# Strassen feed-forward layer: a fourth second-level product in block 0, twelve weight sums moved into block 1, and x of block 2 fetched sooner

## Chip, cores, metric

One NeuronCore of a Trainium2 chip. The metric is the device time of one execution in microseconds (us), the median over several executions. The reported time is some 2 us more than the span of the profile, which ends with the last instruction.

## The reference

```python
batch, m, k, h, n = 16, 512, 768, 3072, 768      # x, w1, b1, w2: normal draws, float32
def reference(x, w1, b1, w2):
    y = np.matmul(x, w1) + b1
    y = 0.5 * y * (1.0 + erf(y / np.sqrt(2.0)))   # exact gelu
    return np.matmul(y, w2).astype(np.float32)
```

The 8192 rows of x are worked in eight blocks of 1024.

## The kernel before

Operands are float16, sums are kept in float32. Every product is done by Strassen's scheme: seven products of half-sized operands in place of eight, for additions that VectorE does beside TensorE. The second products (`gelu(...) @ w2`) of blocks 2 to 7 use two levels of it. Blocks 0 and 1 run while W2 is still being prepared and use one level, with exceptions:

- A **plain unit** (`Unit2`) makes 128 rows of each half of the block's outputs: up to seven products, each of 12 matmuls of 384 columns. A block has four such units.
- A **second-level unit** (`UnitH`) does one whole first-level product of a block by seven products of its own, each of 12 matmuls of 192 columns. It needs sums of the left operand ("level sums", 1536 elements to a partition) and sums of W2's quarters (1152 elements to a partition, 288 KB each).
- In block 1 the first-level products 1, 4 and 2 were second-level units, and its four plain units are **lean**: they do only products 3, 5, 6 and 7.

All of on-chip memory is one tile, `arena`, cut by hand into regions that are reused as soon as their data are dead. So the profile names nearly every on-chip operand "arena", and the scheduler makes an instruction wait whenever it writes a region that an earlier instruction or transfer still uses. Only matmul banks in PSUM have names of their own: bX, bY, bZ, bW.

The sums of W2's quarters for blocks 2 to 7 are stored to DRAM once, in the time of blocks 0 and 1. A sum is written to a staging buffer by VectorE and stored from there by the SP queue:

```python
def split_w2(p, t=None, q=None):          # before: t picked from five staging buffers in turn
    b11, b12, b21, b22 = quarters(p)
    def put(q, src):
        nc.sync.dma_start(out=w2s[p, q][:], in_=src)
    ...
    for n, a, b in ((7, b22, b12), (5, b12, b11), (6, b22, t[5]), (4, b21, t[6])):
        def f(n=n, a=a, b=b):
            tt(t[n], a, b, SUB)                    # VectorE
            puts.append(lambda: put(n, t[n]))      # store, issued at the next slot
        later(WB, f, slow if q is None else q)
```

A unit is a sequence of seven products; between them "slots" 1 to 6 issue other work. The parts that the change touches:

```python
class Unit2:
    def mm(self, p, dst, first, c0, c1):
        if self.lean and p in (1, 2, 4):
            return
        ...
HYBRID = (1, 4, 2)                                 # second-level products, all of block 1
def p7(u):
    u.mm(7, bY[u.g % 2], False, 0, u.C)
    add_c22(u)                                     # VectorE: out row sum, reads bank bY
def p4(u):
    ...
    u.mm(4, bY[u.g % 2], False, 0, u.C)            # goes on in bY: must wait for add_c22
def fill_mm2_one(sb, U, slot):                     # block 0
    ...
            for p in (5, 6, 7, 3):
                split_w2(p)
            hyb_w[1] = split_w2(1)
def fill_hyb(sb, m, slot):                         # second-level units
    ...
    if slot == 6:
        flush(queue)
        if m == 2:
            load_next_x(2, range(3))               # x of block 2, POOL queue, float32 to float16
def fill_lean(sb, k, slot):                        # lean units of block 1
    ...
    if k == 0 and slot == 6:
        for t in range(3):
            transpose_dma(2, t)                    # SP queue
        load_next_x(2, range(3, 6))
    if k == 1 and slot == 2:
        for n in range(2):
            load_wt(2 * NH + n)                    # w1 tiles of block 2, SP queue
    ...
    if k == 3 and slot == 4:
        x_sums(2, soon)
```

## Time and profile before

| | before |
|---|---|
| median time | 852.79 us (852.54 to 854.39, 6 runs) |
| span of the profiled run | 850.6 us |
| matmuls | 6432, TensorE busy 845.5 us |
| block 0's second product to block 2's first matmul | 120.01 to 224.67 us: 104.66 us |
| mean granted clock of TensorE | 1.00 |

The last but one row is the stretch to which the change belongs. It is read as the start of the first matmul of 384 columns of block 0 and the start of the first matmul of 512 columns of block 2.

(Timeline: start, length, engine, line, operation, operands, count, and in brackets the idle time before it and what ended it.)

### The profile page before, as it was taken

Reading aid. Unit: us, or ns where it says so; the run is one execution under the profiler, and the core shown is the slowest. Engines: PE = TensorE matmul, PEld = TensorE weight load, DVE = VectorE, ACT = ScalarE, POOL = GpSimd, SP = SyncE. Lnnn points to the kernel's source line nnn. Section 1 sums busy time; section 2 is a strip of 40 time slices with the busy share of each in tenths; the row PEclk is TensorE's granted clock in tenths of the full one; section 3 lists DMA queues with packets and bytes.
Section 4 is the critical chain, followed back from the end, with each engine's and each line's share of the span. In section 5 each row is a group of like instructions: output and inputs, shape, how many; then the busy total and the mean of one; then the engine's idle time right before and its main releaser. Section 6 shows DMA issues by size and latency. Waiting matters only on the chain.

```text
span 850.6 us, 16487 instructions
## 1 busy us (share of the span) xinstructions
PE 845.5 (99%) x6432; PEld 569.6 (67%) x6432; DVE 667.2 (78%) x1126; ACT 421.3 (50%) x686; POOL 84.1 (10%) x135
## 2 busy tenths in 40 slices
PE   9999999999999999999999999999999999999998
PEld 5444446687544897449964499645995469944798
DVE  5766678786657998679976799768996699956998
ACT  4777761122277513773148822487216771267611
POOL 5021100002100002000020000210002100010000
PEclk9999999999999999999999999999999999999999
DMA  9998777659999699987999689995999949984398
GB/s 229 199 284 170 165 160 277 234 195 218 234 331 207 194 332 372 296 177 236 332 381 266 155 291 335 361 293 111 315 351 344 283 111 328 356 311 172 101 310 283
DMA packets 143522, 219.05 MB, mean 258 GB/s; under 512 B 61756, under 2 KB 84724, under 8 KB 143444
## 3 DMA queue, kind: packets, MB, share of 16 engines
q1 hardware_dynamic: 117824, 179.74, 67.3%
q0 software_dynamic: 25440, 38.15, 20.6%
q8 instruction: 50, 0.82, 0.4%
q14 instruction: 28, 0.23, 0.1%
q10 hardware_dynamic: 180, 0.11, 0.0%
HBM read 180.30 MB, written 47.87 MB: 268 GB/s over the span
## 4 chain that ended last, share of the span: by engine, by line
PE 95%; DMA 4%; DVE 0%; ACT 0%; issue 0%; POOL 0%; DVEq 0%; ACTq 0%
PE bY L388 21%; PE bY L493 15%; PE bX L388 14%; PE bX L493 10%; PE bZ L388 7%; PE bW L388 7%; PE bZ L493 5%; PE bW L493 5%; PE bY L432 5%; DMA arena<-in_x_dram 2%; PE bZ L432 2%; PE bW L432 2%; PE bX L432 2%; DMA arena<-in_w_dram 1%; PE bY L580 1%; PE bX L580 1%
## 5 line engine op out<-in xcount | busy, mean ns | idle before, releaser
L191 DVE TENSOR_TENSOR arena<-arena 128x768 f16<-128x768 f16 (+4 forms) x630 | 403.4, 671 | 7.5 <-PE bW L432 1.1
L388 PEld LDWEIGHTS <-arena 128*128 128x128 f16 x1974 | 192.6, 98 | 224.0 <-issue 0.4
L493 PEld LDWEIGHTS <-arena 128*128 128x128 f16 x3528 | 292.1, 98 | 8.4 <-issue 0.4
L388 PE MATMUL bY<-arena 128*128 128x512 f16 x846 | 214.4, 379 | 0.1
L613 DVE TENSOR_TENSOR arena<-bY,arena 128x512 f32<-128x512 f32 (+1 forms) x102 | 69.4, 681 | 127.0 <-PE bY L388 90.3
L493 PE MATMUL bY<-arena 128*128 128x192 f16 x1500 | 138.3, 246 | 0.0
L388 PE MATMUL bX<-arena 128*128 128x512 f16 x564 | 138.2, 379 | 0.0
L606 ACT COPY bY<-bX 128x512 f32<-128x512 f32 (+1 forms) x143 | 78.6, 550 | 119.4 <-DVE arena L542 82.0
L404 ACT ACTIVATE arena<-arena,b1t 128x1024 f16<-128x1024 f32 x94 | 108.0, 1149 | 54.0 <-DVE arena L641 54.0
L626 ACT COPY arena<-bW 128x512 f32<-128x512 f32 (+1 forms) x147 | 81.1, 552 | 90.7 <-PE bW L493 43.9
L493 PE MATMUL bX<-arena 128*128 128x192 f16 x1020 | 93.1, 246 | 0.1
L641 DVE TENSOR_TENSOR arena<-bZ,arena 128x512 f32<-128x512 f32 (+1 forms) x102 | 69.3, 679 | 22.2 <-PE bZ L388 18.2
L388 PE MATMUL bW<-arena 128*128 128x512 f16 x282 | 76.2, 379 | 0.0
L388 PE MATMUL bZ<-arena 128*128 128x512 f16 x282 | 76.2, 379 | 0.0
L432 PEld LDWEIGHTS <-arena 128*128 128x128 f16 x528 | 51.6, 98 | 34.1 <-issue 0.2
L525 POOL DMA_DIRECT2D out_dram<-arena x42 | 30.6, 729 | 406.4 <-DVE arena L637 370.2
L409 ACT ACTIVATE arena<-bX,b1t 128x512 f16<-128x512 f32 x94 | 64.0, 681 | 10.0 <-PE bX L388 10.0
L409 ACT ACTIVATE arena<-bY,b1t 128x512 f16<-128x512 f32 x94 | 63.4, 674 | 0.0
L657 ACT COPY bZ<-bY 128x512 f32<-128x512 f32 (+1 forms) x54 | 29.0, 537 | 65.7 <-DVE arena L641 31.4
L299 POOL DMA_DIRECT2D arena<-in_x_dram x60 | 32.7, 550 | 248.2 <-DMA arena<-arena 137.9
L493 PE MATMUL bW<-arena 128*128 128x192 f16 x504 | 48.4, 246 | 0.0
L493 PE MATMUL bZ<-arena 128*128 128x192 f16 x504 | 48.4, 246 | 0.0
(60 smaller groups left out, 401.8 us busy)
## 6 DMA issues: line engine op xcount, KB each, us to landing
arena<-w2s SPq DMA_DIRECT2D x294, 288.0 KB, 4.7
arena<-w1s SPq DMA_DIRECT2D x72, 672.0 KB, 7.0
out_dram<-arena POOLq DMA_DIRECT2D x42, 384.0 KB, 7.2
w2s<-arena SPq DMA_DIRECT2D x49, 288.0 KB, 3.8
arena<-in_x_dram POOLq DMA_DIRECT2D x60, 192.0 KB, 7.1
w1s<-arena SPq DMA_DIRECT2D x12, 672.0 KB, 6.1
arena<-in_w_dram POOLq DMA_DIRECT2D x17, 384.0 KB, 7.6
out_dram<-arena SPq DMA_DIRECT2D x17, 384.0 KB, 3.4
```

The lines of the kernel that those rows point to most:

```text
L191: nc.vector.tensor_tensor(out=o, in0=a, in1=b, op=op)
L299: nc.gpsimd.dma_start(out=xhs[t], in_=xr[:, sb * 8 + t, :])
L388: nc.tensor.matmul(out=dst[:, 0:RH], lhsT=w1_op(self.wt, slot)[:, c, :], rhs=a[:, c, :], start=first and c == 0, stop=c == self.C - 1, ski ...
L404: nc.scalar.activation(out=self.G[1][:, hi, :, :], in_=self.tmp, func=GELU, bias=b1t[:, 2 * hi + 1:2 * hi + 2])
L409: nc.scalar.activation(out=self.G[0][:, hi, row, :], in_=bank[:, 0:RH], func=GELU, bias=b1t[:, 2 * hi:2 * hi + 1])
L432: nc.tensor.matmul(out=dst[:, 0:N2], lhsT=a, rhs=w[:, :, c, :], start=first and c == 0, stop=c == self.C - 1, skip_group_check=True)
L493: nc.tensor.matmul(out=dst[:, t * N4:(t + 1) * N4], lhsT=a, rhs=w[:, c, :], start=first and c == 0 and t == ts[0], stop=c == NQ - 1, skip_ ...
L525: eng.dma_start(out=orr[:, s0:s0 + 2, right * N2:(right + 1) * N2], in_=self.dst[:, r].rearrange("p t h n -> p t (h n)"))
L606: nc.scalar.copy(out=bY[u.g % 2][:, 0:u.F], in_=bX[u.g % 2][:, 0:u.F])
L613: nc.vector.tensor_tensor(out=u.c22(), in0=bY[u.g % 2][:, 0:u.F], in1=w[:, 0:u.F], op=ADD)
L626: nc.scalar.copy(out=w[:, 0:u.F], in_=bW[:, 0:u.F])
L641: nc.vector.tensor_tensor(out=u.c12(), in0=bZ[:, 0:u.F], in1=w[:, 0:u.F], op=ADD)
```

## The change

The intent is fewer matmul columns: product 2 of block 0 becomes a second-level unit as well. To make room on VectorE in block 0, twelve of W2's 28 sums move into block 1's units. That costs staging memory: two of the sums' sets share two buffers, and six sums that the second-level units need are stored to DRAM and read back. x of block 2 comes sooner: in the program its first three loads stand two units sooner, its later loads and its transposes about one. Core of the diff:

```diff
-        HYBRID = (1, 4, 2)
+        HYBRID = ((0, 2), (1, 1), (1, 4), (1, 2))          # (block, product)
 # Unit2.mm
-                if self.lean and p in (1, 2, 4):
+                if p == 2 or self.lean and p in (1, 4):
 # p6: copy of a bank in block 0's units goes from VectorE to ScalarE
-            on_act = ... or (isinstance(u, Unit2) and u.lean) or ...
+            on_act = ... or isinstance(u, Unit2) or ...
 # fill_mm2_one (block 0)
-                    for p in (5, 6, 7, 3):
-                        split_w2(p)
-                    hyb_w[1] = split_w2(1)
+                    for p, t in ((6, (0, 1, 2, 3)), (1, (4, 5, 0, 1)), (4, (2, 3, 4, 5)), (2, (0, 1, 2, 5))):
+                        split_w2(p, t)
 # fill_hyb (second-level units)
+            if m == 0 and slot == 1:
+                load_w2s(1, (7, 4))                        # read back
+            if m == 1 and slot == 6:
+                split_w2(7, (6, 7, 6, 7))                  # buffers 6 and 7 for both sets
+                split_w2(5, (6, 7, 6, 7))
+            if (m, slot) in ((1, 6), (2, 1), (2, 3), (2, 5), (3, 1), (3, 4)):
+                slow.pop(0)[1]()                           # one sum of W2 each
+            if m == 2 and slot == 1:
+                load_w2s(4, (7, 4))
             if slot == 6:
                 flush(queue)
-                if m == 2:
+                if m == 1:
                     load_next_x(2, range(3))
+                if m == 3:
+                    for t in range(3):
+                        transpose_dma(2, t)
+                    load_next_x(2, range(3, 6))
 # fill_lean
+            if k == 0 and slot == 4:
+                LAG[0] = 3                                 # stores from here on: three slots after the sum
+                split_w2(3, (1, 2, 3, 4))
-            if k == 1 and slot == 4:
+            if k == 0 and slot == 6:
                 for t in range(3, 6):
                     transpose_dma(2, t)
                 load_next_x(2, range(6, 8))
-            if k == 2 and slot == 4:
+            if k == 1 and slot == 6:
                 for t in range(6, 8):
                     transpose_dma(2, t)
-            if k == 3 and slot == 4:
+            if k == 3 and slot == 3:
                 x_sums(2, soon)
 ...   # buffers' places, output rows split in two, hyb_lev (places of level sums)
```

## The prediction

> **What bounds the kernel now.** I read the page's first part, then the chain that ended last, then the busy time by stage around the second products of blocks 0 and 1 (120 to 225 us, where all of the change lies), then the pieces of the chain and VectorE's timeline there.
>
> ```profile
> PE 845.5 (99%) x6432; PEld 569.6 (67%) x6432; DVE 667.2 (78%) x1126; ACT 421.3 (50%) x686; POOL 84.1 (10%) x135
> ...
> PE 95%; DMA 4%; DVE 0%; ACT 0%; issue 0%; POOL 0%; DVEq 0%; ACTq 0%
> ```
> ```profile
> core 0: us, PE busy (x) PEld busy (x) DVE busy (x) ACT busy (x) POOL busy (x), PEclk, DMA share, GB/s
> 120.00:170.70 50.70, 50.70 (x311) 30.23 (x309) 39.51 (x57) 9.66 (x19) 0.00 (x0) 1.00 0.68 240
> 170.70:194.40 23.70, 23.70 (x253) 21.36 (x252) 20.09 (x28) 6.94 (x15) 1.61 (x3) 1.00 0.56 190
> 194.40:224.70 30.30, 30.30 (x207) 19.43 (x205) 19.18 (x27) 4.92 (x11) 6.71 (x12) 1.00 0.99 207
> ```
>
> TensorE carries 95% of the chain, and in all three stages (block 0's plain units, the three second-level units, the lean units of block 1) its busy time equals the stage. "Busy" overlaps and could hide gaps, so the chain, whose pieces follow each other, is the better proof:
>
> ```profile
> 170.86 0.99 PE bX L580 x12
> 171.85 1.95 PE bY L432 x12
> ...
> 193.54 0.99 PE bX L580 x12
> 194.53 1.02 PE bY L580 x12
> ...
> 224.84 0.65 PE bX L388 x3
> 225.48 2.01 PE bY L432 x12
> ```
>
> Twelve matmuls of 384 columns take 1.95 us (162.5 ns each), twelve of 192 take 0.99 us (82.5 ns). Every piece I compared has that length except two: the product before 195.56 is 0.03 long, the one at 225.48 is 0.06 long. So the region that the change touches holds about 0.1 us of stall. It is pure matmul streaming: time goes down only by the matmuls' columns, and up only by new waits.
>
> **What the Trainium skill says.** "TensorE: Matmul & The Clock Gate", section "Back-to-back issue gap", gives N/2.4 + 2.5 ns at full clock: 162.5 ns for 384 and 82.5 for 192, which is what this trace shows, at a granted clock of 1.00. Its other sentence there, that a stream of weight loads and matmuls of 512 columns sustains some 131 ns each, does not hold here: three of them take 0.65 us, 216 ns each. The same page's "Architectural detail" says VectorE and ScalarE are strict FIFO; so a VectorE sum that has to wait for a buffer holds up the PSUM additions behind it, which matters below. "DMA: Bandwidth & Descriptors", section "Anatomy of one DMA", gives a fixed part of about 2 us per transfer (measured on the GpSimd path); here a 288 KB store of a W2 sum from the SP queue takes 2.1 us at least and 3.7 at the median from 117 to 240 us.
>
> **The change, part by part.**
>
> (a) TensorE. Four plain units lose product 2: 4 x 12 matmuls of 384 columns = 48 x 162.5 = 7.80 us. The new second-level unit has 7 products of 6 x 2 matmuls of 192 columns = 84 x 82.5 = 6.93 us. Net -0.87 us, with 36 more matmuls (6432 to 6468). This is on the path and sure. Per matmul column the second level saves an eighth, but 84 fixed parts of 2.5 ns instead of 48 take back 0.09.
>
> (b) VectorE, rates from its timeline: a 1536-element f16 sum occupies it for 0.88 us (0.95 long, overlapping the next), a 1152-element sum 0.74, a 384-column PSUM addition 0.47. Added: four level sums of the left operand (3.5 us) and some eight small PSUM operations of the new unit; gone: four copies of a bank, which move to ScalarE (4 x 0.47 us; it is 19% busy there). The number of W2 sums is the same, 28 of 0.74 us, but twelve of them (products 7, 5, 3) now run in the units of block 1, five of these between 179 and 193 us. For a plain unit of now 6 x 1.95 = 11.7 us I count 4 operand sums, 6 W2 sums and 2 additions: 3.5 + 4.4 + 0.9 = 8.9 us, in the third unit 10.7 with two level sums. So block 0 has room.
>
> (c) DMA. Six pieces of W2 sums of 288 KB (four of product 1, two of product 4) are stored and read back for the second-level units: 1.7 MB more, in a stage with DMA share 0.56. Lateness counts only at first use. The tightest: product 1's piece 5 can be loaded only when the last plain unit has used its operand (product 3 ends at about 168.8 us), and is wanted 5.9 us later (0.99 + 1.95 + 3 x 0.99). Ahead of it on the queue are one addition (0.6), an output store and its own issue (0.35 each), then 3 to 4 to landing: 4.3 to 5.3 us, so it should just be hidden.
>
> (d) x of block 2 is loaded and transposed sooner, and x's sums go to slot 3 of the last lean unit. That can remove at most the 0.06 at 225.48.
>
> **Where a new wait could appear.** VectorE before, at the end of the second-level units:
>
> ```profile
> 192.46 0.55 DVE L637 TENSOR_TENSOR arena<-bZ,arena 128x384 f32<-128x384 f32 x1
> 192.93 0.95 DVE L191 TENSOR_TENSOR arena<-arena 128x1536 f16<-128x1536 f16 x1
> 193.79 0.56 DVE L654 TENSOR_TENSOR bZ<-bY,arena 128x384 f32<-128x384 f32 x1
> 194.57 0.56 DVE L542 TENSOR_TENSOR arena<-bX,arena 128x384 f32<-128x384 f32 x1 [0.22 <-PE bX L580]
> ```
>
> The addition at 193.79 has to end before TensorE writes bank bY again at 194.4: it is just late, the one 0.03 us stall. Afterwards the same point is at 193.5 us (0.87 sooner). Laying the new order out with the rates of (b): the chain of additions tied to matmuls releases VectorE at 188.75 us (the addition after the second product of the last unit but one); from there to the end of the critical addition stand three PSUM additions (the first at 188.75), one W2 sum, two operand sums and the critical addition itself: 4 x 0.47 + 0.74 + 2 x 0.88 + 0.1 = 4.5, ending at 193.2. Slack 0.3 us if no W2 sum waits for its staging buffer. But the sums of products 7 and 5 share two buffers, and each waits for the store of the last but one: a sum done at 183.05 is stored by 186.2 to 187.3, the next sum in that buffer can start then, and with the level sum behind it VectorE is free at 187.9 to 188.9 instead of 186.8. That just touches 188.75. So I expect a stall of 0 to 0.5 us there, 0.2 in the middle.
>
> **Rivals.**
>
> (1) The stores hold VectorE, and through it TensorE, at several points: 1 to 2 us of stall, which eats the gain: 852.5 to 853.5. For it: VectorE ran without a break from 185 to 190 us before, the stores wait in order on one SP queue behind output stores and read-backs, and two buffers replace five. Against: each sum has a slot of 2 to 3 products before the next use, and DMA is idle half of that stage.
>
> (2) A read-back is late: TensorE waits at the second unit's product 5 or the third's product 7, 0.5 to 1.5 us each: also 852.5 to 853.5. For it: a median of 4.7 us from issue to landing for such loads over the whole kernel. Against: that median is of busy stages; 288 KB stores here land in 2.7 us at the median between 170 and 200 us.
>
> (3) Earlier x and the lighter block 0 give more than I count, by a better phase of the later blocks: 851 or less. Against: the later blocks stream just as tightly (one is 103.25 us long, between the first second-level products at 291.11 and 394.36, of which 102.9 is matmul columns by the same rates), so there is 0.3 us a block to win and nothing in the change aims at it.
>
> A stage that becomes VectorE-bound as a whole I leave out: 39.5 of 50.7 us, less the copies, plus the level sums, is no bound.
>
> **Range and chances.** 852.62 - 0.87 + 0.2 (stall at the critical addition) - 0.05 (x sooner) = 851.9 us. Rivals 1 and 2 together, perhaps one chance in four, add about 1; the runs before spread from 852.54 to 854.39, so a median can move up by some tenths or, with two slow starts of three, by over 1 us. I take 851.0 to 853.2. 2% is 17 us, twenty times the largest effect; nothing here can cost that short of a program that was built wrong: 0.98 for within 2%.
>
> **What would show it right or wrong.** The chain of the changed kernel should have 84 more matmuls of 192 columns and 48 fewer of 384 in that region, still 0.99 and 1.95 us a dozen, and block 2's first matmul should start 0.6 to 0.9 us sooner than 224.67. The stall, if any, should be on bY at about 193.5 us, ended by VectorE's addition to bZ, and VectorE before it idle for a store of W2 sums. I am wrong if TensorE waits for a DMA at a second-level unit's product 5 or 7, if a piece of the chain in block 0 is long, or if block 2's first matmul starts later than before; and wrong on the size if the change of the start at 224.67 and that of the whole time differ by more than 0.5 us.

## More of the kernel before

The stage of the second-level units is the one to keep in mind. Here are three pieces of it, in the view of busy time by stretch; the columns are stretch, its length, busy time (and number of instructions) of PE (TensorE's matmuls), PEld (its weight loads), DVE (VectorE), ACT (ScalarE) and POOL (GpSimd), granted clock of TensorE, share of the DMA engines' time (times of packets are summed, so it can pass 1), GB/s.

```profile
184.00:192.00 8.00, 8.00 (x100) 8.00 (x98) 7.53 (x12) 2.52 (x6) 0.54 (x1) 1.00 0.38 115
192.00:195.00 3.00, 3.00 (x39) 2.98 (x37) 2.78 (x5) 0.96 (x2) 1.07 (x2) 1.00 0.93 193
195.00:202.80 7.80, 7.80 (x65) 5.67 (x63) 5.45 (x8) 1.43 (x3) 1.94 (x3) 1.00 1.10 164
```

TensorE is never idle here.

The DMA engines are used for 38% from 184 to 192 us and wholly after that, because the first three loads of x of block 2 begin only at 189.96 us:

```profile
189.96 0.54 POOL L299 DMA_DIRECT2D arena<-in_x_dram  x1 [78.42 <-PE bY L580]
```

The bracket matters: the load waits for a second-level matmul, since it lands where a level sum of that unit lies.

## The result

| | before | after |
|---|---|---|
| median time, us | 852.79 (852.54 to 854.39) | 857.36 (856.62 to 861.57) |
| span of the profiled run, us | 850.6 | 857.2 |
| block 0's second product to block 2's first matmul | 104.66 us | 110.17 us (119.94 to 230.11) |

The ratio is 1.0059, with a 95% interval of 1.0037 to 1.0081, from six fast runs of each. Ratios here are the mean time of one kernel's fast runs over that of the other's of the same rounds, so not quite the ratio of the medians quoted. The change made the kernel slower by 0.6%, where 0.1% faster was predicted; the time lies above the predicted 851.0 to 853.2 us. Numbers of lines are those of the changed kernel from here on: L452 is a plain unit's matmul (L432 before), L599 a second-level unit's (L580 before), L408 one of a first product (L388 before).

TensorE's total, from the page of the changed kernel:

```profile
PE 847.2 (99%) x6468; PEld 573.8 (67%) x6468; DVE 670.9 (78%) x1132; ACT 423.0 (49%) x692; POOL 85.5 (10%) x139
```

The 36 more matmuls are there, and yet busy time rose by 1.7 us, where the columns alone should have taken 0.87 us off it. The same three stretches as above, now of the changed kernel:

```profile
184.00:192.00 8.00, 7.62 (x93) 7.39 (x90) 1.14 (x2) 2.36 (x5) 0.00 (x0) 1.00 0.90 217
192.00:195.00 3.00, 0.02 (x1) 0.11 (x2) 2.17 (x4) 0.00 (x0) 0.00 (x0) 0.85 0.20 80
195.00:202.80 7.80, 7.80 (x49) 6.46 (x49) 6.28 (x10) 0.96 (x2) 0.00 (x0) 0.62 0.40 120
```

Three things to see, in order of time. From 184 to 192 us the DMA engines are 90% busy instead of 38%, and VectorE does almost nothing (1.14 us of 8, 7.53 before). From 192 to 195 us TensorE stands still. From 195 to 202.8 us it is "busy" all the time and yet does 49 matmuls where it did 65, at a granted clock of 0.62: busy time grew because the matmuls were slow.

What VectorE waited for, in its timeline:

```profile
184.48 0.76 DVE L205 TENSOR_TENSOR arena<-arena 128x1152 f16<-128x1152 f16 x1
192.83 1.63 DVE L205 TENSOR_TENSOR arena<-arena 128x1152 f16<-128x1152 f16 x2 [7.59 <-DMA w2s<-arena]
194.38 0.55 DVE L623 TENSOR_TENSOR arena<-bY,arena 128x384 f32<-128x384 f32 x1
```

The sums of 1152 elements are sums of W2. (A merged line shows the form of its first instruction: the two at 192.83 are a sum of W2 and a level sum.) The one at 192.83 writes a staging buffer whose last sum has to be stored first, and waited 7.59 us for that store. L623 is the addition `add_c22` of the third second-level unit; it reads a bank that TensorE had finished at about 188.5 us (product 7 started at 187.49), but stands behind the held sum in VectorE's order. The chain that ended last passes through the store after that one, issued at 185.27, which was late too: it landed 8.16 us later, at 193.43 (start, length, what):

```profile
185.27 8.16 DMA w2s<-arena
...
194.38 0.56 DVE arena L623
194.94 0.04 issue
194.98 2.08 PE bY L599 x12
```

And TensorE's timeline there (lengths overlap a little; differences of starts are the true lengths):

```profile
190.46 1.15 PE L599 MATMUL bY<-arena 128*128 128x192 f16 x12
194.98 2.08 PE L599 MATMUL bY<-arena 128*128 128x192 f16 x12 [3.37 <-DVE arena L623]
196.85 2.12 PE L599 MATMUL bX<-arena 128*128 128x192 f16 x12
198.79 2.11 PE L599 MATMUL bY<-arena 128*128 128x192 f16 x12
200.69 2.25 PE L452 MATMUL bW<-arena 128*128 128x384 f16 x12
202.78 1.15 PE L599 MATMUL bZ<-arena 128*128 128x192 f16 x12
```

A dozen of 192 columns, 0.99 us before the stall, takes 1.87 us, then 1.94 and 1.90. The dozen of 384 columns takes 2.09 instead of 1.95; at 202.78 the full rate is back. Not all of this is the clock's: the dozen at 198.79 needed VectorE's addition to bank bZ, and VectorE, after its hold of 7.59 us, came to that addition only now (its timeline):

```profile
198.18 0.56 DVE L666 TENSOR_TENSOR bZ<-bY,arena 128x384 f32<-128x384 f32 x1
```

It ended at 198.74, so at full clock the dozen at 198.79 would hardly have started sooner.

Next, what ran beside the slow store; that it is the cause is tested below (e6, e7). The stores of W2 sums issued from 178 to 196 us, five, took 2.1 us from issue to landing at the least, 5.8 at the median and 9.7 at the most, as far as they landed in that stretch (before the change: 2.1, 4.3 and 5.0); the slowest is the one that VectorE waited for, issued at 183.07. The two read-backs among them took 5.9 and 10.2 us; the later, issued at 181.8, landed near 192.0, 0.6 us after the stalled product was due, so without VectorE's hold TensorE would have waited for it a little. The three loads of x, at 189.96 us before, now start here:

```profile
180.96 1.63 POOL L313 DMA_DIRECT2D arena<-in_x_dram  x3
```

There is no bracket: nothing held them. From 178 to 196 us POOL's queue, which carries these loads and four output stores, took 36.7% of the DMA engines' time.

There is a second stall, at the start of block 2, again in the chain:

```profile
220.52 9.01 DMA out_dram<-arena
...
231.62 0.47 ACT bZ L669
232.10 0.04 issue
232.14 2.11 PE bY L452 x12
```

An output store took 9 us to land; VectorE's addition behind it (4.48 us idle) was late, then ScalarE's copy of bank bZ, then product 7 of the last lean unit. That dozen starts 1.38 us after the matmuls before it end, where before the change it was 0.07. On the SP queue the loads of w1 for block 2 had slipped from 200.23 us to just ahead of this store. SP's own timeline, before and after, and from its waits in the changed kernel what held the loads:

```profile
200.23 1.01 SPq L219 DMA_DIRECT2D arena<-w1s  x2
```
```profile
219.03 0.88 SPq L233 DMA_DIRECT2D arena<-w1s  x2
...
220.52 0.64 SPq L480 DMA_DIRECT2D out_dram<-arena  x1
```
```profile
SPq L233 <- DMA w2s<-arena: 4.2, 1, 4.2
```

They waited 4.2 us for the store of a W2 sum, and the output stores stood behind them.

Sum for the profiled run, each from starts in the timelines:

- matmul columns: -0.87 us
- stall before product 4 of the third second-level unit: that dozen was due at 190.46 + 0.99 = 191.45 and came at 194.98: +3.53
- half rate from 194.98 to 202.78: 7.80 us for 3 x 0.99 + 1.95 = 4.92 us of matmuls: +2.88, of which 1.83 until 198.79, when VectorE's addition would have held TensorE at full clock too, and 1.05 after it (1.90 - 0.99 and 2.09 - 1.95), which is the clock's own
- together +5.54; block 2's first matmul came 110.17 - 104.66 = 5.51 later, counted from block 0's second product
- stall at the start of block 2: 1.38 - 0.07 = +1.31

The total of 6.8 is close to the 6.6 by which the spans differ. The profiled run is one of the two slow ones of six: its mean clock was 0.995 and its span 857.2 us. The spans of the others were 854.8, 855.2, 854.9 and 855.9 at clocks of 0.997 to 1.000, and 859.8 at 0.995. So the half rate is not in every run to the same degree; runs without a profile do not show more. The two at a clock of 1.000 are still 4.3 and 4.6 us longer than the kernel before, so most of the loss is not the clock's.

### The profile page after: what moved, and what is told of

Read it like the earlier page. It is cut to its first block, busy times and chain, and to the rows that moved or that the text cites. A ratio compares the mean times of both kernels' runs of the same rounds, so it can differ in the third digit from the quotient of the medians.

```text
span 857.2 us, 16585 instructions
## 1 busy us (share of the span) xinstructions
PE 847.2 (99%) x6468; PEld 573.8 (67%) x6468; DVE 670.9 (78%) x1132; ACT 423.0 (49%) x692; POOL 85.5 (10%) x139
## 4 chain that ended last, share of the span: by engine, by line
PE 95%; DMA 4%; DVE 1%; issue 0%; POOL 0%; ACT 0%; DVEq 0%; SPq 0%; ACTq 0%
PE bY L408 21%; PE bY L512 14%; PE bX L408 14%; PE bX L512 10%; PE bZ L408 7%; PE bW L408 7%; PE bZ L512 5%; PE bW L512 5%; PE bY L452 4%; PE bW L452 2%; PE bZ L452 1%; DMA w2s<-arena 1%; DMA arena<-in_x_dram 1%; DMA out_dram<-arena 1%; PE bY L599 1%; PE bX L452 1%
## 5 line engine op out<-in xcount | busy, mean ns | idle before, releaser
L205 DVE TENSOR_TENSOR arena<-arena 128x1536 f16<-128x1536 f16 (+6 forms) x634 | 406.0, 671 | 14.2 <-DMA w2s<-arena 7.6
L408 PEld LDWEIGHTS <-arena 128*128 128x128 f16 x1974 | 192.5, 98 | 223.9 <-issue 0.2
L408 PE MATMUL bY<-arena 128*128 128x512 f16 x846 | 214.4, 379 | 0.0
L408 PE MATMUL bX<-arena 128*128 128x512 f16 x564 | 138.2, 379 | 0.0
L408 PE MATMUL bW<-arena 128*128 128x512 f16 x282 | 76.2, 379 | 0.0
L408 PE MATMUL bZ<-arena 128*128 128x512 f16 x282 | 76.2, 379 | 0.0
L452 PEld LDWEIGHTS <-arena 128*128 128x128 f16 x480 | 47.0, 98 | 32.4 <-issue 0.9
L669 ACT COPY bZ<-bY 128x512 f32<-128x512 f32 (+1 forms) x58 | 30.8, 532 | 76.3 <-DVE arena L653 34.8
## 6 DMA issues: line engine op xcount, KB each, us to landing
arena<-in_x_dram POOLq DMA_DIRECT2D x60, 192.0 KB, 7.1
```

The costliest lines, as they stand in the source:

```text
L205: nc.vector.tensor_tensor(out=o, in0=a, in1=b, op=op)
L408: nc.tensor.matmul(out=dst[:, 0:RH], lhsT=w1_op(self.wt, slot)[:, c, :], rhs=a[:, c, :], start=first and c == 0, stop=c == self.C - 1, ski ...
L452: nc.tensor.matmul(out=dst[:, 0:N2], lhsT=a, rhs=w[:, :, c, :], start=first and c == 0, stop=c == self.C - 1, skip_group_check=True)
L669: nc.scalar.copy(out=bZ[:, 0:u.F], in_=bY[u.g % 2][:, 0:u.F])
```

## The experiments

Theory at the outset: x, loaded 9 us sooner, fills the DMA engines just when VectorE needs two staging buffers back; the late store holds VectorE, VectorE holds TensorE, and the idle time costs clock. Rivals: (R1) the two buffers are too few whatever x does, so the traffic is innocent; (R2) the half-rate stretch is the larger cost and has a cause of its own. Runs of one call are on the same chip, and "before" below is the median of the kernel before in that call.

### x back to its old place in the program (e1)

```diff
 # fill_hyb, slot 6
-                if m == 1:
+                if m == 3:
                     load_next_x(2, range(3))
-                if m == 3:
-                    for t in range(3):
-                        transpose_dma(2, t)
-                    load_next_x(2, range(3, 6))
 # fill_lean
             if k == 0 and slot == 6:
+                for t in range(3):
+                    transpose_dma(2, t)
+                load_next_x(2, range(3, 6))
+            if k == 1 and slot == 4:
                 for t in range(3, 6):
 ...
-            if k == 1 and slot == 6:
+            if k == 2 and slot == 4:
 ...
-            if k == 3 and slot == 3:
+            if k == 3 and slot == 4:
```

> x of block 2 loaded and transposed as in the kernel before, all else as changed. Theory (the three early x loads crowd the DMA engines, so the store of a W2 sum lands 10 us after its issue and VectorE waits for its staging buffer): the stores between 180 and 195 us land in under 5 us, the 3.4 us stall before the third second-level unit's product 4 goes, the clock stays at 1.000, 851.9 to 852.8 us. Rival (two staging buffers are too few whatever the traffic): a stall of 2 us or more stays there, 855 us or more.

Measured: 862.34 us (859.46 to 865.49), before 852.75; ratio 1.011 (1.0093 to 1.0128). Slower still, and the theory was not tested, because the three loads did not move. POOL's timeline of this run:

```profile
181.40 1.63 POOL L313 DMA_DIRECT2D arena<-in_x_dram  x3
```

The loads come last in the program but first in time: POOL has nothing else to do, and in the changed kernel's memory plan the places where x lands are free by then. Before, it was a level sum in that place that held them, not their position in the program. What did move was the transposes and the later loads, on which block 2's sums of x depend: a new wait of 3.7 us for such a sum, and the second stall grew to 2.0. A fault of the experiment, and a lesson: look at what holds a transfer before moving its line.

### Six staging buffers in place of two (e2)

```diff
-    spare = stage + [wb_at(2 * XT_N + PAR + k * WB) for k in range(2)]
+    spare = stage + [wb_at(2 * XT_N + PAR + k * WB) for k in range(6)]
-                split_w2(7, (6, 7, 6, 7))
-                split_w2(5, (6, 7, 6, 7))
+                split_w2(7, (6, 7, 8, 9))
+                split_w2(5, (10, 11, 3, 4))
```

Memory of block 0's dead activations gives four more buffers; with two older ones, 3 and 4, each of the eight sums has its own and none waits for a store.

> x early as changed, but the W2 sums of products 7 and 5 get eight different staging buffers instead of two. Theory (late store held VectorE only through the buffer): the stores still land late (8 us or more), but VectorE does not wait for them, the stall goes, and so does the wait of the w1 load for the last of these stores at block 2's start: 851.9 to 853. Rival (VectorE is simply short of time there, or the late stores hurt another way): 855 us or more.

Measured: 852.83 us (852.1 to 854.14), before 852.75; ratio 1.0004 (0.9992 to 1.0016); result correct. The stores still took up to 9.4 us to land, but VectorE did not wait for them:

```profile
184.50 2.41 DVE L205 TENSOR_TENSOR arena<-arena 128x1152 f16<-128x1152 f16 x3
188.94 0.56 DVE L623 TENSOR_TENSOR arena<-bY,arena 128x384 f32<-128x384 f32 x1 [2.03 <-ACT bY L618]
```

(VectorE's timeline.) Three sums run in a row at 184.50 and the addition comes in time at 188.94, 5.4 us sooner than in the changed kernel. The first stall, the half rate and the second stall are all gone; 0.25 us of waiting for a read-back remains before product 4 (0.42 by the starts; the view counts matmuls as 0.17 us longer, here and in the waits quoted below), and block 2's first matmul is 104.19 us after block 0's second product, 0.47 less than before. So the path from slow store to stall goes through the two buffers. This alone does not say why the stores are slow.

### A filler against the lower clock (e3)

```diff
+            if isinstance(u, UnitH) and u.p == 4:
+                for n in range(24):
+                    nc.tensor.matmul(out=bX[u.g % 2][:, 0:N4], lhsT=ident[:],
+                                     rhs=u.w[1][:, 0, :], start=True, stop=True,
+                                     skip_group_check=True)
```

Two dozen matmuls whose results are overwritten keep TensorE busy in the stall.

> The changed kernel with 24 useless matmuls of 192 columns (about 2 us) into a free bank just before the stalled product, so that TensorE is idle for 1.5 us at a stretch and not 3.5. Theory (the half-rate matmuls after the stall are a clock drop that the long idle time sets off, in some runs only): granted clock 1.000 in every run, the median at the level of the changed kernel's runs with clock 1.000, 856.6 to 857.0, and none at 859 or above. Rival (the clock drops for another reason): clocks of 0.995 to 0.998 still appear, or the filler adds its 2 us.

Measured: 859.99 us (858.18 to 861.1), before 852.75; ratio 1.0091 (1.0078 to 1.0104). The expected gain did not come. One of its five runs still has a mean clock of 0.998, so not even that part of the expectation held throughout. The profile (span 856.4) shows no matmul at half rate, the granted clock from 195 to 203 us is 1.00, but TensorE waits twice; in the view of waits (who for whom: us in total, times, longest):

```profile
PE bY L599 <- DVE bZ L671: 1.7, 1, 1.7
...
PE bY L599 <- DVE arena L623: 0.8, 1, 0.8
```

After the hold VectorE is itself behind: its addition to bank bZ came at 198.62 us, and product 7 had to wait for it until 199.24. In the changed kernel the slow matmuls ran in just that time. Block 2's first matmul came 108.75 us after block 0's second product, 1.42 less than in the changed kernel's profile, not 2.9; but the second profile of the changed kernel (e5 below) has 108.60 without a filler, so the difference of two profiles does not measure the clock. The changed kernel's own trace does so better: 1.05 of the 2.88 us, the rest lies beside VectorE's lateness. R2 is weakened: the clock follows from the stall (e2, e6 and e7, without that stall, have 1.00 there) and is worth less than it looks. The other four runs of the filler were slower than the profiled one and have no profile; why, stays open.

### Both (e4)

Edit: those of e1 and e2 together.

> x late and separate staging buffers together. Theory: no stall of over 0.3 us at the third second-level unit and the full 0.87 us of the matmuls gained: 851.6 to 852.2. If the part of the change on TensorE alone is worth less than worked out, it stays at 852.5 or more.

Measured: 857.75 us (855.57 to 861.1), ratio 1.0061 (1.0047 to 1.0076). The first stall is gone as in e2; e1's wait for a sum of x remains at block 2 (1.8 us), and one of 1.2 for a w1 tile is new. The expected 851.6 to 852.2 was missed: e1's half spoils it.

### The changed kernel again (e5)

> The changed kernel as it is, as the control on the chip and in the job of the next three. No theory says other than 856.5 to 858; with the 7 to 8 us hold of VectorE for the store of a W2 sum.

No edit: a control on another chip. Measured: 859.73 us (857.58 to 860.75), before 852.63; ratio 1.0076 (1.0062 to 1.009). VectorE was held 6.90 us, TensorE stalled 2.69 and then 2.26 us, the clock from 195 to 202 us was 0.76. Block 2's first matmul came after 108.60 us. The slowing is not one chip's, and on this one the time is above the expected 856.5 to 858.

### x held back as before (e6)

```diff
-               [strip(0, 1, 0, 2 * P), strip(0, 0, NQ, 2 * P), strip(0, 1, NQ, 2 * P), strip(0, 0, 0, 0)],
+               [strip(0, 1, 0, 2 * P), strip(0, 0, NQ, 2 * P), strip(1, 1, NQ, 0), strip(0, 0, 0, 0)],
-                lev_sums(None, m=2)
+                lev_sums(None, m=2, ks=(0, 1, 3))
+            if m == 1 and slot == 4:
+                lev_sums(None, m=2, ks=(2,))
+            if m == 3 and slot == 1:
+                load_next_x(2, (1, 2, 0))
-                if m == 1:
-                    load_next_x(2, range(3))
```

A level sum is placed where x lands, as it was in the kernel before, and the loads are issued behind it. The buffers stay two.

> Two staging buffers as changed; the first three x loads are held by their data until the third second-level unit's product 7 is done (about 188.6 us, instead of 181), because one level sum is put where x lands; transposes and later loads as changed. In the first try (x moved in the program only) the loads still went out at 181.4, so it did not test this. Theory (the x loads crowd out the store of the W2 sum): the store that took 10 us lands in under 5, VectorE's hold shrinks below 2 us, and the stall before product 4 goes or stays under 0.5 us: 852.0 to 854. Rival (the hold does not come from x): hold of 5 us or more, 856 or more.

Measured: 856.11 us (854.66 to 857.26), before 852.63; ratio 1.0038 (1.0025 to 1.005). POOL's timeline, then VectorE's:

```profile
189.12 1.62 POOL L313 DMA_DIRECT2D arena<-in_x_dram  x3 [7.81 <-PE bY L599]
```
```profile
187.11 1.63 DVE L205 TENSOR_TENSOR arena<-arena 128x1152 f16<-128x1152 f16 x2 [1.72 <-DMA w2s<-arena]
```

Now the loads wait for the matmul (bracket), the stores of W2 sums land in 2.1, 3.0 and 4.0 us (least, median, most), VectorE's hold is 1.72 us instead of 7.59, and TensorE has no first stall. (The control, e5, had a hold of 6.90.) Block 2's first matmul comes 103.80 us after block 0's second product: all of the predicted 0.87 us. This speaks for the theory and against R1 as the whole cause: two buffers suffice if x keeps away. But the second stall grew, as the timeline of TensorE shows:

```profile
228.11 3.46 PE L452 MATMUL bY<-arena 128*128 128x384 f16 x12 [3.22 <-ACT bZ L669]
```

It is 3.22 us, followed by a dozen that took 3.29 us to the next start instead of 1.95. Its chain again begins at an output store, issued at 215.33 us and landed 10.16 later. So the time missed its expected 852.0 to 854 and lies where the rival put it, but by the second stall and not by the rival's hold. x's traffic was taken out of 181 to 189 us and put beside the stores of W2 sums that are now in block 1; that this made the output store late is likely, and not tested by itself.

### x's early loads made thin (e7)

```diff
-            nc.gpsimd.dma_start(out=xhs[t], in_=xr[:, sb * 8 + t, :])
+            c = 8 if sb == 2 and t < 3 else K
+            nc.gpsimd.dma_start(out=xhs[t][:, 0:c], in_=xr[:, sb * 8 + t, 0:c])
```

> Wrong results on purpose: the first three x loads of block 2 bring 8 columns of 768, at their changed places, so that only their traffic is gone. Theory: as for the held x, hold below 2 us, no stall over 0.5 us at product 4: 852.0 to 853.5. Rival (other traffic, the read-backs or the unit's own output stores, holds the store): hold stays at 5 us or more, 856 or more.

Measured: 852.99 us (852.7 to 853.53), before 852.63; ratio 1.0004 (0.9991 to 1.0016). The loads are issued at the changed kernel's place (182.14 us) and everything else is the changed kernel's, but they move hardly any data. The stores land in 2.1, 3.3 and 4.7 us (least, median, most) and the hold shrinks, though not below the expected 2 us (VectorE's timeline):

```profile
188.99 1.63 DVE L205 TENSOR_TENSOR arena<-arena 128x1152 f16<-128x1152 f16 x2 [2.76 <-DMA w2s<-arena]
```

The stall before product 4 is gone; 0.2 us remains two dozens later, at the addition to bZ, and 0.6 at block 2's start. Same instructions, same waits, same two buffers, less traffic: it is the bytes of the early x that made the store late. This is the cleanest of the tests.

### Held x with six buffers (e8)

Edit: those of e6 and e2 together.

> x held to 188.6 us and separate staging buffers together. Theory: neither the hold nor the late read-back of product 4's piece (0.4 us with separate buffers alone) is left, so the 0.87 us shows: 851.5 to 852.3, faster than before by about 0.1%. If the held x makes block 2's sums late instead, 853 or more with a wait at block 2's start.

Measured: 853.5 us (852.93 to 854.47), ratio 1.0011 (0.9999 to 1.0024), but with a relative error of 0.086, unintended: an extra buffer overlaps the level sum that e6 moved (e10 leaves it out and is correct). Its time is indicative only and no conclusion rests on it.

### What makes the second stall (e9, e10, e11)

e9 is e6 with two other buffers for the sums of product 5, so that the w1 tile, which lies over buffer 7, need not wait for their stores:

```diff
-                split_w2(5, (6, 7, 6, 7))
+                split_w2(5, (6, 7, 3, 4))
```

e11 is e9 with the first two w1 loads issued ahead of the transposes of x:

```diff
-            if k == 1 and slot == 2:
+            if k == 0 and slot == 5:
```

e10 is e11's order with e8's buffers laid clear of the level sum.

Expected of e9:

> x held as in the run before, and the last two sums of product 5 in buffers that the w1 tiles of block 2 do not overlap. Second stall (product 7 of the last lean unit, 3.2 us with x held): if it comes from the w1 loads waiting for the store of a W2 sum and holding output stores behind them on the SP queue, it shrinks below 1 us and the time is 852 to 853. Rival: the w1 loads are late because the x transposes stand ahead of them, and it is their traffic that makes the output store land 10 us after issue; then the stall stays at 1.5 us or more, 854 or more.

of e10:

> x held, w1 first, and five more staging buffers for the sums of products 7 and 5, chosen so that none overlaps the level sum (the earlier try with six and x held overlapped it and gave a wrong result). Best candidate: all of the 0.87 us of matmuls and no new stall, 851.6 to 852.1. If block 2's third unit waits for its w1 tile as in the earlier try (1.5 us), 853 or more.

of e11 ("the run before" is e9):

> As the run before, and the first two w1 loads of block 2 issued ahead of x transposes 3 to 5 (near 200 us, as in the kernel before, instead of 212). If their place behind the transposes is what makes the output store late: second stall under 0.5 us, 851.7 to 852.5. If the transposes or x loads alone make it late: the stall stays over 1 us, 853.5 or more.

Measured, before 852.79:

| | median us | ratio | TensorE's waits around block 2's start |
|---|---|---|---|
| e9 | 853.59 (853.39 to 855.63) | 1.0014 (1.0002 to 1.0027) | 1.47 (ScalarE's copy of bZ), 1.44 (w1 tile) |
| e10 | 854.76 (854.22 to 855.87) | 1.0020 (1.0006 to 1.0034) | 0.77 (VectorE's copy to bZ), 1.47 (w1 tile) |
| e11 | 855.03 (853.88 to 856.4) | 1.0024 (1.0012 to 1.0037) | 1.33 (VectorE's copy to bZ), 1.17 (w1 tile) |

In e9 the w1 loads no longer wait for a store and the second stall is halved from 3.22 to 1.47, not below 1 as expected; its time fits neither branch. In e11 that stall is gone, but VectorE waits 2.14 us for a transpose of x at 226.41, so the sums of x and its later copy to bZ are late; from its view of waits:

```profile
PE bX L408 <- DMA arena<-w1s: 1.5, 2, 1.2
PE bY L408 <- DVE bZ L671: 1.3, 1, 1.3
```

The times hoped for in e10 and e11 (851.6 to 852.1, 851.7 to 852.5) were both missed. So the order of the SP queue and the buffer under the w1 tile are both part of it, and with x held back every order tried only moves the wait. The DMA engines' share from 200 to 225 us is 0.97 in the kernel before and 1.02 to 1.06 in the changed kernel, e6 and e9, and 0.92 to 0.93 in e10 and e11, which still wait. In e2 and e12, where x is early and no sum waits for a buffer, the share is as high (1.06 and 1.04), the w1 loads go out at 210.2 and 209.8 us, and there is no second stall. So the share by itself does not tell whether TensorE waits. How much of the second stall each contributor makes was not separated.

### Six buffers, read-backs first (e12)

```diff
-    spare = stage + [wb_at(2 * XT_N + PAR + k * WB) for k in range(2)]
+    spare = stage + [wb_at(2 * XT_N + PAR + k * WB) for k in range(6)]
-                split_w2(7, (6, 7, 6, 7))
-                split_w2(5, (6, 7, 6, 7))
+                split_w2(7, (6, 7, 8, 9))
+                split_w2(5, (10, 11, 3, 4))
+            if m == 1 and slot == 4:
+                load_w2s(4, (7, 4))
             if m == 2 and slot == 1:
-                load_w2s(4, (7, 4))
 ...
-            if k == 3 and slot == 5:
+            if k == 3 and slot == 3:
```

From e2: the two read-backs whose lateness left 0.25 us go ahead, at 175.9 us, and two w1 loads go out two slots sooner.

> The six-buffer version with x early (852.83 before) and two more moves on the SP queue: the two read-backs of product 4 issued as soon as their buffer is free, ahead of the store of a W2 sum (near 179 us, before the x loads), and the next two w1 tiles ahead of two output stores. Its two remaining waits were 0.4 us (product 4, for a read-back) and 0.2 us (second tile of block 2). If these were what hid the gain: 851.9 to 852.4, with no wait of TensorE over 0.1 us from 120 to 250 us. If the w1 tiles now delay the output stores instead: 852.7 or more, with a wait on bZ's copy at block 2's start.

Measured: 852.14 us (851.76 to 852.87), before 852.72; ratio 0.9993 (0.9980 to 1.0007); result correct. Its chain through the stretch has no gap any more; these are its first piece of 384 columns and the first two pieces at block 2:

```profile
120.19 1.95 PE bX L452 x12
...
223.99 0.65 PE bX L408 x3
224.64 2.01 PE bY L452 x12
```

From 120.19 to 223.99 us are 103.80, where the kernel before has 104.67 between the same pieces (120.17 to 224.84). All of the 0.87 us is there, with x as early as in the changed kernel and both stalls gone. The whole time is 0.6 us lower by the medians, within the noise by the interval. It is the best version found; that it beats the kernel before is likely from the profile, not proven by the times. Its slowest store of a W2 sum from 178 to 196 us took 7.5 us, against 9.4 in e2, where the read-backs ran beside it: they seem to have a smaller part in the slow stores.

## Why the prediction was wrong

**What bounds the kernel, and step (a), the columns: right.** TensorE's streaming is the bound, a hole in it goes straight into the time, and the second level in block 0 is worth 0.87 us: e6 and e12 both measure it.

**Step (b), VectorE's room in block 0: right.** No piece of TensorE's chain there is long; from 120 to 171 us TensorE is busy throughout, with VectorE busy for 42.5 of the 51 us (39.8 before).

**Step (c), the DMA traffic: right in what it counted, and it counted the wrong thing.** The tight read-back that it worked out (product 1's) made no wait. The other one that rival 2 named (the third unit's, for its product 4 rather than 7) cost 0.42 us in e2, and in the changed kernel its 0.6 us lay hidden beside VectorE's hold: rival 2 came true in part.

**Step (d), x sooner: the step that failed.** It credited the earlier loads with at most 0.06 us and charged them nothing. It took a new place in the program for an earlier time and did not ask when the loads would start or beside what: 9.0 us sooner (180.96 instead of 189.96), among the W2 stores, the output stores and the read-backs. "DMA is idle half of that stage", held against rival 1, was read from the trace of before, where x came only near the end of that stage. Nor did the early loads bring much: the first transposes of x start at 195.22 us before and at 194.62 in e12, where nothing stalls; in the changed kernel, in SP's order behind W2 stores that are held up, at 199.85.

**The stall at bank bY, 0.2 us in the middle: right place and mechanism, wrong size.** The prediction said that a W2 sum would wait for its staging buffer and that VectorE would hold TensorE at bY near 193.5 us; it happened at bY, until 194.98, but through the addition `add_c22` and at product 4 of the third unit, two dozens of matmuls before the piece that was named. The mis-sized term is the landing time of one store: a sum done at 183.05 "is stored by 186.2 to 187.3", 3.1 to 4.3 us. (The 3.7 us that it read as the median for a W2 sum's store mixes two kinds of store: for the 28 sums alone the view has 2.1, 2.9 and 5.0. That is not what went wrong.) The trace has the store issued at 183.07 and landed 9.7 us later, so the term is 9.7 us, and the stall 3.53 us. With thin x (e7) the slowest store took 4.7 us and a stall of 0.2 came at bY, ended by the addition to bZ, just as predicted: on its own assumption the sum was good. VectorE's strict order, which it took from the skill, is what the trace shows: `add_c22`, whose bank was ready at about 188.5, ran at 194.38, behind the held sum. The step that set the assumption failed, not the arithmetic after it. The Trainium skill has what was overlooked: "DMA: Bandwidth & Descriptors", section "Issuing engines are not separate DMA queues", says that transfers started by different engines run on the same 16 DMA engines and interleave. e6 and e7 agree with it: the loads are on POOL's queue and the stores on SP's, and yet the slowest store lands in 4.0 us with the loads out of the way (e6), 9.7 with them.

**The rivals.** Rival 1 was the right one and was put at 1 to 2 us; it measured 3.5, and what follows from it is more. None of the rivals had the lower clock. "TensorE: Matmul & The Clock Gate", section "What's actually happening", says that the array's clock is halved after an idle window of about 3.4 us and that the window runs freely. The trace agrees: clock 0.57 from 195 to 202 us after 3.5 us of stall. The stretch cost 2.88 us in the profiled run, of which 1.83 lay beside VectorE's lateness. None of the rivals had the second stall either, 1.3 us: the W2 sums moved into block 1 put stores on the SP queue, whose transfers are issued in order, just ahead of block 2, and one of their buffers lies under a w1 tile. e9 shows the second of these at work.

**The range.** It allowed for rivals of 1 us. A stall of more than ten times its middle estimate, because one landing time depends on what else is moving, was the risk to be put into the range; the prediction knew that its slack of 0.3 us hung on that landing time and should have asked what could make it 10. The sign that it had named itself, block 2's first matmul later than before, came: 230.11 us, not 224.67.

## What to carry to other kernels

A moved load brings its bytes to the new time: before moving it, find what holds it now (a buffer or a queue, often not its place in the program), work out when it will really start, and count what it will share the DMA engines with. Where an in-order engine fills few staging buffers, the landing time of a store under load, not alone, decides whether it stands still, and everything behind it stands too. A stall on TensorE can cost more than its length: here 3.5 us of it were followed by 6 us at half the clock, though only 1 us of that was the clock's own cost, since VectorE was late as well.

## What the Trainium skill lacked or had wrong

- "DMA: Bandwidth & Descriptors": it gives the time of a transfer by itself and says that transfers interleave, but no landing time for one beside others. Here a 288 KB store landed in 2.1 us at the least and in 9.7 us beside three loads of x (192 KB each where they land) and two read-backs, at a DMA share of 0.90 from 184 to 192 us; with the loads of x held back the slowest took 4.0 us.
- "TensorE: Matmul & The Clock Gate": the idle window of about 3.4 us is not a safe limit for a single stall. After stalls of 2.69 us (e5) and 2.68 us (e1) the granted clock from 195 to 202 us was already down to 0.76 and 0.79, and after e1's second stall, 1.96 us, it was 0.59 from 231.5 to 235.
- The same page's sustained rate of some 131 ns for matmuls of 512 columns was not seen: three of them take 0.65 us, 216 ns each, before and after, which is the figure that the page gives for an isolated matmul only.
